# Two dilated blocks handled together, scores four blocks ahead, in a two-layer attention kernel

## The chip, the cores and the metric

The kernel runs on one core of a Trainium2 chip. The metric is device time in microseconds of one execution of the whole program. PE is TensorE (PEld its weight loads), DVE is VectorE, ACT is ScalarE, POOL is GpSimd and SP is SyncE, which issues nearly all DMAs here.

## The reference

Two layers, each with one input projection, two token mixers that read it, a gate, and one output projection. The change touches the second mixer alone: 12 heads of 64, 2048 tokens, three (window, dilation) patterns.

```
for window, dilation in ((128, 1), (512, 4), (2048, 16)):
    # queries and keys are cut into 128-token blocks per residue class of the dilation;
    # a block of queries sees its own block of keys and the one before (masked to the window)
    s = q_block @ [k_prev, k_own].T * scale ; s = where(mask, s, -inf)
    m = max(s) ; p = exp(s - m) ; l = sum(p)
    o = (p @ [v_prev, v_own]) / l ; log_den = m + log(l)
alpha = softmax(log_den over the three patterns)
od = sum(alpha * o over the three patterns) * silu(gate)
```

## The kernel before, in words

Each layer runs four stages one after the other: projection, stick-breaking mixer (`_stick`), dilated mixer (`_dilated`), output projection (`_output`, whose first loads are mixed into the end of the dilated stage). Heads are taken two at a time, so the dilated mixer has 6 pairs. A pair has 48 blocks: 16 for each pattern p. Blocks are numbered g over all pairs; t is g within its pair. In pattern 0 every block uses its own keys only (128 columns of scores, "own-key blocks"); in patterns 1 and 2 a block has 256 columns of scores unless it is the first of its residue class.

Three functions make a block:

- `front(g)`: four score matmuls on PE (L742) into one of three PSUM banks; for each of the two heads DVE adds the mask and takes the row minimum while moving the scores out of PSUM (L744), and ACT takes the exponential with its row sum (L748).
- `mid(g)`: PE transposes the weights of the block (L763; two transposes in an own-key or first block, four otherwise) into one of two PSUM banks, and one copy moves them out (L765), on ACT for one block in four, otherwise on DVE.
- `back(g0)`: for the four blocks from g0, the matmuls with the values (L777; 128x64 weights, two instructions each) into one PSUM bank, which ACT copies out (L782, L784 or L787).

The loop takes one block in each step: `front(g + 3)`, then (in later pairs) one weighting of the pair before, then `mid(g)`, and every fourth step `back(g - 4)`. `tc.keep_in_program_order` (called `pin`) fixes this order on PE. The other engines' queues are in the order that the tile framework's planner gives them; each engine then runs its queue in order.

Once a pair is done its three outputs are mixed, while the next pair runs. `stats_a` (t = 1) and `stats_b` (t = 5) turn the row minima and sums into weights for the three patterns, a chain that goes PE, ACT, DVE, POOL, ACT, POOL, DVE (a reciprocal, L832) and POOL again. `weigh(c)` spreads the weights of one sixteenth of the tokens over the partitions with one matmul (L847) and multiplies them in on DVE (L848); it runs at t = 17 to 32, one per block. After every fourth one `gate` adds the three patterns and multiplies by the gate on POOL (L855 to L858), and `put` (t = 26, 30, 34, 38) stores a quarter through SP. `load_v`, `load_k` and `load_q` bring the next data through SP, and `make_q` reorders the queries on POOL (L682, L686) for patterns 1 and 2.

The buffers that the change touches are `pe_s`, which holds the exponentials of a block between `front` and `mid` (five slots), and `ts_s`, which holds its transposes between `mid` and `back` (five slots). Scores rotate over three banks, transposes over two, weightings over two.

Of the kernel before, what the change touches and what calls it, by code (L numbers as in the profile page):

```python
# [20 lines left out]
NT = 16  # L21
NK = DM // 128
NPAIR = 6
# [468 lines left out]
def _stick(tc, mem, sq_scr, sb_scr, g_scr, mix, ident):  # L492
# [28 lines left out]
    def load_vn(pr):  # L521
        vn[pr] = mem.get(("F5", "F6")[pr], [128, NT, 128])
        nc.sync.dma_start(out=vn[pr], in_=sb_scr[:, 128 * pr:128 * pr + 128].rearrange("(j p) d -> p j d", p=128))

    def load_gt(pr):
        gt[pr] = mem.get(("F8", "F7")[pr], [128, NT, 128])
        nc.sync.dma_start(out=gt[pr], in_=g_scr[pr].rearrange("p (c a) -> p c a", c=NT))
# [62 lines left out]
    def back(u):  # L590
# [11 lines left out]
        if lo == 0 and i % 4 == 0:  # L602
# [3 lines left out]
            if i == 0:  # L606
                nc.sync.dma_start(out=mix[0][pr].rearrange("p (c a) -> p c a", c=NT), in_=gt[pr])

    LEAD, BATCH = 2, 4
    later = {2: lambda: load_gt(0), 8: lambda: load_vn(1), 12: lambda: load_gt(1),  # L610
             16: lambda: prep(1, 1), 20: lambda: prep(1, 0)}
    for u in range(LEAD):
        front(u)
    done = 0
    for u in range(len(units)):
        if u + LEAD < len(units):
            front(u + LEAD)
        mid(u)
# [12 lines left out]
def _dilated(tc, mem, v_scr, qk_scr, g_scr, mix, masks, sel, ident, neg1):  # L631
    nc = tc.nc
    pin = tc.keep_in_program_order
# [3 lines left out]
    t_r = mem.bank_ring(3, 4)  # L637
    o_r = mem.bank_ring(5)
    w_r = mem.bank_ring(6, 7)
    pa, pb = mem.get("H0", [128, 2, 2, 256]), mem.get("H1", [128, 2, 2, 256])  # L640
    ta, tb = mem.get("H6", [128, 2, 2, 2, 128]), mem.get("H7", [128, 1024])
    pe_s = Slices([pa[:, 0], pa[:, 1], pb[:, 0], pb[:, 1], tb[:, 512:1024].rearrange("p (h k) -> p h k", h=2)])
    td = mem.get("H5", [128, 2, 2, 2, 128])
    ts_s = Slices([td[:, 0], td[:, 1], ta[:, 0], ta[:, 1], tb[:, 0:512].rearrange("p (c h q) -> p c h q", c=2, h=2)])
    xa = mem.get("X", [128, 1024])
    gt_r = mem.ring("S0", "S1")
    st_r = mem.ring("T0", "T1")
# [19 lines left out]
    def load_q(pr):  # L667
        qq[pr] = [[], []]
        for h in range(2):
            t = q_r.get([128, S])  # L670
            nc.sync.dma_start(out=t, in_=qk_scr[pr, h])
            qq[pr][h].append(t)
# [33 lines left out]
    for i in range(4):  # L706
        t = gt_r.get([128, 4, 128])
# [5 lines left out]
    def geom(p, b):  # L713
        if p == 0:
            return b, 0, True
        c, n = (b // 4, b % 4) if p == 1 else (0, b)
        return c, n, n == 0

    def front(g):
        pr, p, b = g // 48, g // 16 % 3, g % 16  # L720
        if (p, b) == (0, 0):
            o3s[pr] = mem.get(f"G{pr % 2}", [128, 3, NT, 128])
            sts[pr] = st_r.get([128, 2, 3, 2, NT])
        st = sts[pr]
        c, n, first = geom(p, b)
        un = 128 if first else 256
        if p:
            run, stp = (32, 4) if p == 1 else (8, 1)
            w0 = 0 if first else run * (n - 1)
        m0 = M_OWN[p] + 128 - un  # L730
        sc = s_r.get([128, 2, 256])
        pe = pe_s.get()
        for h in range(2):
            qb = qq[pr][h][p].bitcast(F32R)[:, 128 * b:128 * b + 128]
            for s in range(2):
                kt = kk[pr][h][s]
                if p == 0:
                    kv = kt[:, 128 * b:128 * b + 128]
                else:
                    kv = kt.rearrange("p (c a) -> p c a", c=NT)[  # L740
                        :, c::stp, w0:w0 + run * un // 128].rearrange("p c (w a) -> p w c a", a=run)
                pin(nc.tensor.matmul(sc[:, h, :un], qb, kv, start=s == 0, stop=s == 1))  # L742
        for h in range(2):
            nc.vector.tensor_tensor_reduce(  # L744
                out=pe[:, h, :un], in0=sc[:, h, :un], in1=mk[:, m0:m0 + un],
                scale=-0.125, scalar=3.0e38, op0=ALU.add, op1=ALU.min,
                accum_out=st[:, 0, p, h, b:b + 1])
            nc.scalar.activation(pe[:, h, :un], pe[:, h, :un], AF.Exp, scale=-1.0,  # L748
                                 bias=st[:, 0, p, h, b:b + 1], accum_out=st[:, 1, p, h, b:b + 1])
        pes[g] = pe  # L750

    pes, tss = {}, {}

    def mid(g):
        p, b = g // 16 % 3, g % 16
        first = geom(p, b)[2]
        pe = pes.pop(g)
        tp = t_r.get([128, 2, 2, 128])
        nch = 1 if first else 2
        for ch in range(nch):  # L760
            for h in range(2):
                w = 0 if first else 1 - ch
                pin(nc.tensor.transpose(tp[:, ch, h], pe[:, h, 128 * w:128 * w + 128], ident))  # L763
        ts = ts_s.get()
        (nc.scalar.copy if g % 4 == 1 else nc.vector.tensor_copy)(ts[:, :nch], tp[:, :nch])  # L765
        tss[g] = ts

    def back(g0):
        pr, p, b0 = g0 // 48, g0 // 16 % 3, g0 % 16
        o3 = o3s[pr]  # L770
        ob = o_r.get([128, 4, 128])
        for b in range(b0, b0 + 4):
            ts = tss.pop(g0 + b - b0)
            nch = 1 if geom(p, b)[2] else 2
            for ch in range(nch):
                for h in range(2):
                    pin(nc.tensor.matmul(  # L777
                        ob[64 * h:64 * h + 64, b % 4],
                        vq[(pr * 3 + p) * 2 + (b - ch) // 8][:, (b - ch) % 8, 64 * h:64 * h + 64], ts[:, ch, h],
                        start=ch == 0, stop=ch == nch - 1))  # L780
        if p == 0:
            nc.scalar.copy(o3[:, 0, b0:b0 + 4], ob)  # L782
        elif p == 1:
            nc.scalar.copy(o3[:, 1, b0 // 4::4].rearrange("p r (n a) -> p n r a", n=4),  # L784
                           ob.rearrange("p n (r a) -> p n r a", r=4))
        else:
            nc.scalar.copy(o3[:, 2, :, 8 * b0:8 * b0 + 32].rearrange("p c (j a) -> p j c a", j=4),  # L787
                           ob.rearrange("p j (c a) -> p j c a", c=NT))
# [51 lines left out]
    def weigh(pr, c):  # L840
        o3 = o3s[pr]
        if c % 4 == 0:
            gts[pr] = gt_r.get([128, 4, 128])
            nc.sync.dma_start(out=gts[pr], in_=g_scr[2 + pr, :, 128 * c:128 * c + 512].rearrange(
                "p (c a) -> p c a", c=4))
        wb = w_r.get([128, 3, 128])
        pin(nc.tensor.matmul(wb, selr[:, c], wr, start=True, stop=True))  # L847
        nc.vector.tensor_tensor(out=o3[:, :, c], in0=o3[:, :, c], in1=wb, op=ALU.mult)  # L848

    def gate(pr, c4, m7=None):  # L850
        final = pr == NPAIR - 1
        cs = slice(4 * c4, 4 * c4 + 4)
        o3, gt = o3s[pr], gts[pr]
        e1 = nc.vector if final and c4 % 2 else nc.gpsimd
        e1.tensor_tensor(out=o3[:, 0, cs], in0=o3[:, 0, cs], in1=o3[:, 1, cs], op=ALU.add)  # L855
        e1.tensor_tensor(out=o3[:, 0, cs], in0=o3[:, 0, cs], in1=o3[:, 2, cs], op=ALU.add)
        o = o3[:, 0, cs]
        e1.tensor_tensor(out=o, in0=o, in1=gt, op=ALU.mult)  # L858
        if final:
            nc.scalar.copy(m7[0][:, cs], o)  # L860
            e1.tensor_tensor(out=m7[1][:, cs], in0=o, in1=m7[0][:, cs].bitcast(F32), op=ALU.subtract)
            if len(mix) > 1:
                put(pr, c4)

    def put(pr, c4):
        nc.sync.dma_start(out=(mix[1][0] if pr == NPAIR - 1 else mix[0][2 + pr])[:, 512 * c4:512 * c4 + 512].rearrange(
            "p (c a) -> p c a", c=4), in_=o3s[pr][:, 0, 4 * c4:4 * c4 + 4])

    LEAD = 3
    total = NPAIR * 48  # L870
    for g in range(LEAD):
        front(g)
    for g in range(total):
        pr, t = g // 48, g % 48
        if t % 8 == 2:
            load_v(g // 8 + 1)
        if t == 2:
            make_q(pr, 2)
        if pr + 1 < NPAIR:
            if t == 16:  # L880
                load_k(pr + 1)
            if t == 24:
                load_q(pr + 1)
            if t == 36:
                make_q(pr + 1, 1)
        if g + LEAD < total:
            front(g + LEAD)
        if pr and 17 <= t < 33:
            weigh(pr - 1, t - 17)
            if t % 4 == 0:  # L890
                gate(pr - 1, (t - 17) // 4)
        mid(g)
        if g % 4 == 0 and g:
            back(g - 4)
        if pr:
            if t == 1:
                stats_a(pr - 1, nc.gpsimd)
            elif t == 5:
                stats_b(pr - 1, nc.gpsimd)
            elif t in (26, 30, 34, 38):  # L900
                put(pr - 1, (t - 26) // 4)
        yield
    back(total - 4)
    m7 = [mem.get("F5", [128, NT, 128], F32R), mem.get("F6", [128, NT, 128], F32R)]
# [108 lines left out]
```

## Time and profile before

| what | value |
|---|---|
| median of 3 runs | 3153.92 us (3147.05 to 4272.47) |
| profiled execution | 3151.59 us, of which the span is 3149.9 us |
| granted TensorE clock, mean | 0.993 |
| busy share of the span | PE 97%, PEld 83%, DVE 49%, ACT 44%, POOL 37% |

The profile is one execution; the span runs from its first instruction to its last. PE's busy time counts pipelined matmuls with modelled ends, so that a full PE is not yet a PE that could go no faster. The order of work inside a stage is read from the timeline, where successive instructions of one line are merged into one row with their count.

### The profile page before, as it was taken

The page shows a single profiled execution, that of the slowest core. Times are in us where ns is not written, and L with a number is a line of the kernel's source. Part 1 is how long each engine was busy: PE and PEld are TensorE (multiplying, and loading weights), DVE is VectorE, ACT ScalarE, POOL GpSimd, SP SyncE. Part 2 cuts the span into 40 slices and gives each one's busy share as a digit, 9 for nine tenths or more (in the row PEclk, how much of TensorE's full clock was granted, in tenths as well). Part 3 has the DMA queues.
Part 4 walks back from the last instruction along what each step waited for, and adds up shares of the span by engine and source line. Part 5 has one row for each costly group of instructions (what it writes and reads, how often), then busy time and mean ns, then how long its engine had stood idle before and what let it go on. Part 6 is the DMA issues. An engine that isn't in the chain of part 4 may idle for free.

```text
span 3149.9 us, 58168 instructions
## 1 busy us (share of the span) xinstructions
PE 3069.2 (97%) x21328; PEld 2615.0 (83%) x21328; DVE 1551.8 (49%) x4035; ACT 1370.4 (44%) x3917; POOL 1170.3 (37%) x1302
## 2 busy tenths in 40 slices
PE   8999999999999999979999999999999999999799
PEld 8888888887778988868898888888877789888687
DVE  6234430013777878864253243301147778888621
ACT  5222221113667888852042122211136688888410
POOL 1056651102663445451010666511036624445500
PEclk9999999999999999989999999999999999999899
DMA  6234456417123566354343344563172236663443
GB/s 200 89 102 121 112 137 199 136 53 227 58 81 95 154 192 176 104 163 145 124 144 104 97 110 119 148 205 119 59 219 61 72 95 177 190 174 102 137 146 99
DMA packets 316891, 413.10 MB, mean 131 GB/s; under 512 B 23232, under 2 KB 248512, under 8 KB 306368
## 3 DMA queue, kind: packets, MB, share of 16 engines
q1 hardware_dynamic: 314304, 405.20, 44.0%
q10 hardware_dynamic: 2304, 4.20, 0.4%
q8 instruction: 170, 2.79, 0.4%
q14 instruction: 113, 0.93, 0.1%
HBM read 252.01 MB, written 157.29 MB: 130 GB/s over the span
## 4 chain that ended last, share of the span: by engine, by line
PE 82%; issue 6%; ACT 4%; DVE 3%; DMA 2%; POOL 2%; SPq 1%; DVEq 0%; POOLq 0%; ACTq 0%
PE b L742 8%; PE b L317 7%; PE b L316 7%; PE b L315 7%; PE b L777 6%; PE b L763 6%; PE b L321 6%; PE b L323 6%; PE b L322 6%; PE b L599 4%; PE b L967 4%; PE b L966 4%; PE b L963 4%; PE b L585 2%; PE b L558 2%
## 5 line engine op out<-in xcount | busy, mean ns | idle before, releaser
L748 ACT ACTIVATE H<-H,T 128x256 f32<-128x256 f32 (+1 forms) x1152 | 519.4, 455 | 74.3 <-DVE T L744 67.8
L744 DVE CUSTOM_DVE_ANT_0 H<-b,M 128x256 f32<-128x256 f32 (+1 forms) x1152 | 370.9, 360 | 110.7 <-PE b L742 41.5
L742 PE MATMUL b<-F,F 128*128 128x256 f32 (+1 forms) x2304 | 408.4, 301 | 3.1 <-DVE T L744 3.1
L317 PE MATMUL b<-F,F 128*128 128x512 f32 (+1 forms) x1152 | 410.0, 356 | 0.5 <-DVE F L288 0.3
L573 POOL TENSOR_TENSOR G<-G 128x512 f32<-128x512 f32 (+3 forms) x320 | 287.7, 911 | 196.5 <-DVE G L567 143.2
L567 DVE TENSOR_TENSOR_SCAN G<-G,b 128x513 f32<-128x513 f32 (+3 forms) x320 | 323.8, 1079 | 73.2 <-ACT G L566 68.1
L742 PEld LDWEIGHTS b<-F,F 128*128 128x128 f32 x2304 | 312.1, 191 | 32.1 <-issue 26.3
L763 PE MATMUL b<-ident,H 128*128 128x128 f32 x1800 | 298.8, 277 | 7.8 <-ACT H L765 5.4
L315 PE MATMUL b<-F,G 128*128 128x512 f32 (+1 forms) x768 | 275.7, 359 | 0.4 <-ACT G L287 0.4
L316 PE MATMUL b<-F,G 128*128 128x512 f32 (+1 forms) x768 | 273.6, 356 | 1.5 <-POOL F L218 1.5
L315 PE MATMUL b<-F,F 128*128 128x512 f32 (+1 forms) x768 | 274.1, 357 | 0.0
L316 PE MATMUL b<-F,F 128*128 128x512 f32 (+1 forms) x768 | 272.3, 355 | 0.0
L317 PEld LDWEIGHTS b<-F,F 128*128 128x128 f32 x1152 | 217.6, 189 | 32.2 <-DVE F L288 1.1
L765 DVE COPY H<-b 128x512 f32<-128x512 f32 (+1 forms) x432 | 241.2, 558 | 4.3 <-PE b L763 4.1
L777 PE MATMUL b<-H,H 128*64 128x128 f32 x3600 | 235.7, 278 | 0.1
L763 PEld LDWEIGHTS b<-ident,H 128*128 128x128 f32 x1800 | 212.2, 141 | 17.7 <-ACT H L765 7.7
L322 PE MATMUL b<-F,F 128*128 128x512 f32 x576 | 224.6, 390 | 0.0
L566 ACT ACTIVATE G<-b 128x512 f32<-128x512 f32 (+3 forms) x320 | 163.9, 559 | 132.3 <-PE b L559 105.9
L777 PEld LDWEIGHTS b<-H,H 128*64 128x64 f32 x3600 | 192.8, 137 | 32.2 <-issue 21.9
L748 ACT ACTIVATION_READ_ACCUMULATOR H<-H,T 128x1 f32 x1152 | 219.5, 191 | 0.0
L135 POOL TENSOR_SCALAR U<-U 128x16 f32<-128x16 f32 (+1 forms) x80 | 18.9, 236 | 536.8 <-DVE U L367 316.3
L963 PE MATMUL b<-F,H 128*128 128x512 f32 x448 | 179.4, 400 | 29.3 <-ACT H L957 29.3
(159 smaller groups left out, 6297.0 us busy)
## 6 DMA issues: line engine op xcount, KB each, us to landing
qk_l<-H SPq DMA_DIRECT2D x384, 128.0 KB
F<-qk_l SPq DMA_DIRECT2D x48, 1024.0 KB
v_l<-S SPq DMA_DIRECT2D x288, 128.0 KB
H<-v_l SPq DMA_DIRECT2D x72, 512.0 KB
F<-qk_l SPq DMA_DIRECT2D x48, 512.0 KB
sq_l<-H SPq DMA_DIRECT2D x64, 256.0 KB
g_l<-S SPq DMA_DIRECT2D x64, 256.0 KB
F<-sq_l SPq DMA_DIRECT2D x32, 512.0 KB
```

The costliest lines, as they stand in the source:

```text
L315: nc.tensor.matmul(ps, hT(q, 0, k)[:, cs], wh, start=k == 0, stop=False)
L316: nc.tensor.matmul(ps, hT(q, 0, k)[:, cs], wl, start=False, stop=False)
L317: nc.tensor.matmul(ps, hT(q, 1, k)[:, cs], wh, start=False, stop=k == NK - 1)
L322: nc.tensor.matmul(ps, wh[:, w], hT(tq, 1, k), start=False, stop=False)
L567: nc.vector.tensor_tensor_scan(out=r[:, 0:n + 1][:, ::-1], data0=g[:, 512 - n:513][:, ::-1], data1=z[:, 0:1].to_broadcast([128, n + 1]), i ...
L573: nc.gpsimd.tensor_tensor(out=b[:, :n], in0=r[:, 1:n + 1], in1=r[:, 0:n], op=ALU.subtract)
L742: pin(nc.tensor.matmul(sc[:, h, :un], qb, kv, start=s == 0, stop=s == 1))
L744: nc.vector.tensor_tensor_reduce(out=pe[:, h, :un], in0=sc[:, h, :un], in1=mk[:, m0:m0 + un], scale=-0.125, scalar=3.0e38, op0=ALU.add, op ...
L748: nc.scalar.activation(pe[:, h, :un], pe[:, h, :un], AF.Exp, scale=-1.0, bias=st[:, 0, p, h, b:b + 1], accum_out=st[:, 1, p, h, b:b + 1])
L763: pin(nc.tensor.transpose(tp[:, ch, h], pe[:, h, 128 * w:128 * w + 128], ident))
L777: pin(nc.tensor.matmul(ob[64 * h:64 * h + 64, b % 4], vq[(pr * 3 + p) * 2 + (b - ch) // 8][:, (b - ch) % 8, 64 * h:64 * h + 64], ts[:, ch, h],
L963: ins = nc.tensor.matmul(ps, h, wo[k][:, 0, ns], start=k == 0, stop=False)
```

## The change

Blocks are handled two at a time: on even g the loop now issues `front` for g + 4 and g + 5, then the weightings, then (every second time) `back(g - 4)`, then `mid` for g and g + 1. Scores thus run four blocks ahead of the transposes (LEAD 4), and the value matmuls stand ahead of the transposes. `pe_s` gets six slots and `ts_s` four. In pattern 0 the transposes of two blocks go into one bank and leave in one copy. The 16 weightings of a pair are spread over t = 16 to 36, three in four blocks (in the last pair two per two blocks, t = 18 to 32). The gates follow the weightings, and the stores move to t = 25, 31, 35, 41 (last pair: 27, 31, 35, 38).

```diff
-    pe_s = Slices([pa[:, 0], pa[:, 1], pb[:, 0], pb[:, 1], tb[:, 512:1024].rearrange("p (h k) -> p h k", h=2)])
+    pe_s = Slices([pa[:, 0], pa[:, 1], pb[:, 0], pb[:, 1]]
+                  + [tb[:, i:i + 512].rearrange("p (h k) -> p h k", h=2) for i in (0, 512)])
     td = mem.get("H5", [128, 2, 2, 2, 128])
-    ts_s = Slices([td[:, 0], td[:, 1], ta[:, 0], ta[:, 1], tb[:, 0:512].rearrange("p (c h q) -> p c h q", c=2, h=2)])
+    ts_s = Slices([td[:, 0], td[:, 1], ta[:, 0], ta[:, 1]])
...
     def mid(g):
-        p, b = g // 16 % 3, g % 16
-        first = geom(p, b)[2]
-        pe = pes.pop(g)
-        tp = t_r.get([128, 2, 2, 128])
-        nch = 1 if first else 2
-        for ch in range(nch):
-            for h in range(2):
-                w = 0 if first else 1 - ch
-                pin(nc.tensor.transpose(tp[:, ch, h], pe[:, h, 128 * w:128 * w + 128], ident))
-        ts = ts_s.get()
-        (nc.scalar.copy if g % 4 == 1 else nc.vector.tensor_copy)(ts[:, :nch], tp[:, :nch])
-        tss[g] = ts
+        both = g // 16 % 3 == 0
+        for i in range(2):
+            first = geom(g // 16 % 3, g % 16 + i)[2]
+            pe = pes.pop(g + i)
+            if i == 0 or not both:
+                tp, ts = t_r.get([128, 2, 2, 128]), ts_s.get()
+            nch = 1 if first else 2
+            lo = i if both else 0
+            for ch in range(nch):
+                for h in range(2):
+                    w = 0 if first else 1 - ch
+                    pin(nc.tensor.transpose(tp[:, lo + ch, h], pe[:, h, 128 * w:128 * w + 128], ident))
+            tss[g + i] = ts[:, lo:lo + nch]
+            if both and i == 0:
+                continue
+            on_act = g % 8 == 2 if both else (g + i) % 4 == 1
+            (nc.scalar.copy if on_act else nc.vector.tensor_copy)(ts[:, :lo + nch], tp[:, :lo + nch])
...
-    LEAD = 3
+    LEAD = 4
...
-        if g + LEAD < total:
-            front(g + LEAD)
-        if pr and 17 <= t < 33:
-            weigh(pr - 1, t - 17)
-            if t % 4 == 0:
-                gate(pr - 1, (t - 17) // 4)
-        mid(g)
-        if g % 4 == 0 and g:
-            back(g - 4)
+        if g % 2 == 0:
+            for i in (0, 1):
+                if g + LEAD + i < total:
+                    front(g + LEAD + i)
+            if pr:
+                cs = range(t - 18, t - 16) if pr == NPAIR - 1 else range(3 * (t - 16) // 4, 3 * (t - 14) // 4)
+                for c in cs:
+                    if 0 <= c < NT:
+                        weigh(pr - 1, c)
+                        if c % 4 == 3:
+                            gate(pr - 1, c // 4)
+            if g % 4 == 0 and g:
+                back(g - 4)
+            mid(g)
...
-            elif t in (26, 30, 34, 38):
-                put(pr - 1, (t - 26) // 4)
+            elif pr == NPAIR - 1 and t in (27, 31, 35, 38):
+                put(pr - 1, (t - 27) // 4 if t < 38 else 3)
+            elif pr < NPAIR - 1 and t in (25, 31, 35, 41):
+                put(pr - 1, (t - 25) // 5)
```

## Rows read from the trace of the kernel before

**Rows 1.** The page: share of the chain that ended last, by engine.
```profile
PE 82%; issue 6%; ACT 4%; DVE 3%; DMA 2%; POOL 2%; SPq 1%; DVEq 0%; POOLq 0%; ACTq 0%
```
**Rows 2.** Windows, layer 0: dilated stage, then tail; length, busy, clock, DMA, GB/s.
```profile
981.00:1374.00 393.00, 388.16 (x4030) 350.53 (x4031) 322.85 (x1452) 339.72 (x1306) 176.64 (x223) 1.00 0.54 153
1374.00:1432.00 58.00, 39.88 (x193) 31.32 (x190) 32.79 (x42) 16.10 (x24) 26.91 (x22) 0.82 0.56 178
```
**Rows 3.** Timeline of PE, first pair, pattern 1: start, length, line, count.
```profile
1006.12 1.75 PE L777 MATMUL b<-H,H 128*64 128x128 f32 x28
1007.80 0.66 PE L742 MATMUL b<-F,F 128*128 128x128 f32 x4
1008.30 0.62 PE L763 MATMUL b<-ident,H 128*128 128x128 f32 x4
1008.68 0.71 PE L742 MATMUL b<-F,F 128*128 128x256 f32 x4
...
1011.06 0.38 PE L763 MATMUL b<-ident,H 128*128 128x128 f32 x2
1011.38 0.33 PE L777 MATMUL b<-H,H 128*64 128x128 f32 x2
```
**Rows 4.** Timeline of PE, fourth pair, the same four blocks with weightings.
```profile
1203.60 1.95 PE L777 MATMUL b<-H,H 128*64 128x128 f32 x28
1205.48 0.66 PE L742 MATMUL b<-F,F 128*128 128x128 f32 x4
...
1209.76 0.33 PE L777 MATMUL b<-H,H 128*64 128x128 f32 x2
```
**Rows 5.** Timeline of PE, value matmuls in pattern 0: first pair, then fourth.
```profile
984.09 1.09 PE L777 MATMUL b<-H,H 128*64 128x128 f32 x16
987.92 1.09 PE L777 MATMUL b<-H,H 128*64 128x128 f32 x16
...
1183.27 1.09 PE L777 MATMUL b<-H,H 128*64 128x128 f32 x16
1187.91 1.10 PE L777 MATMUL b<-H,H 128*64 128x128 f32 x16
```
**Rows 6.** Windows: pattern 0 (first pair); weightings; pattern 2. Order PE PEld DVE ACT POOL.
```profile
984.10:995.90 11.80, 11.79 (x122) 10.69 (x121) 8.62 (x55) 11.80 (x56) 2.28 (x4) 1.00 0.76 194
1197.40:1216.10 18.70, 18.70 (x187) 16.77 (x186) 18.17 (x72) 14.82 (x55) 12.35 (x15) 1.00 0.55 177
1222.00:1239.00 17.00, 17.00 (x187) 16.03 (x186) 13.42 (x58) 14.92 (x55) 8.28 (x12) 1.00 0.44 137
```
**Rows 7.** Timeline of DVE and PE, third pair, where the weights are made.
```profile
1118.96 0.94 DVE L832 RECIPROCAL X<-X 32x128 f32<-32x128 f32 x1 [1.42 <-POOL X L831]
...
1120.32 0.66 PE L742 MATMUL b<-F,F 128*128 128x128 f32 x4 [0.50 <-DVE T L744]
```
**Rows 8.** Groups by form, evictions of transposes: count, busy us, mean ns, idle before.
```profile
L765 DVE COPY H<-b 128x512 f32<-128x512 f32 x228 | 156.1, 685 | 4.1 <-PE b L763 4.1
L765 DVE COPY H<-b 128x256 f32<-128x256 f32 x204 | 85.1, 417 | 0.2
L765 ACT COPY H<-b 128x512 f32<-128x512 f32 x96 | 55.3, 576 | 13.8 <-PE b L763 13.6
L765 ACT COPY H<-b 128x256 f32<-128x256 f32 x48 | 17.5, 365 | 2.4 <-PE b L763 2.4
```
**Rows 9.** Timeline of DVE, fourth pair, one block with a weighting.
```profile
1202.40 0.68 DVE L765 COPY H<-b 128x512 f32<-128x512 f32 x1
1203.00 0.41 DVE L744 CUSTOM_DVE_ANT_0 H<-b,M 128x256 f32<-128x256 f32 x1
...
1203.34 0.42 DVE L744 CUSTOM_DVE_ANT_0 H<-b,M 128x256 f32<-128x256 f32 x1
...
1203.68 0.55 DVE L848 TENSOR_TENSOR G<-G,b 128x384 f32<-128x384 f32 x1
1204.15 0.68 DVE L765 COPY H<-b 128x512 f32<-128x512 f32 x1
```

## The prediction

> **What bounds the kernel now.** I read the chain that ended last first: PE holds 82% of it, ACT 4%, DVE 3% [rows 1]. So only what shortens PE's own sequence, or a wait inside it, can move the end. The windows by stage come next: a dilated stage takes 393 us and its twin in the second layer about as long, a quarter of the span together; PE is busy 388 of the 393 at the full clock [rows 2]. Since busy PE may hide waiting, I then compared the same four blocks in a pair without weightings and in one with them, in PE's timeline. In the first pair four blocks of pattern 1 take 1011.38 - 1006.12 = 5.26 us: 1.68 from the first value matmul to the next score, 3.58 for the four steps of scores and transposes [rows 3]. With four weightings they take 6.16: 1.88 and 4.28 [rows 4]. So a weighting costs PE (4.28 - 3.58) / 4 = 0.18 us of its own, and the value matmuls lose 0.20 in their run, where they wait for the copy of the last block's transposes. DVE is why: it is busy 18.17 of 18.70 us there, against 13.42 of 17.00 in pattern 2 without weightings [rows 6].
>
> Pattern 0 is different. In the first pair four own-key blocks take 3.83 us [rows 5], and ACT is busy all 11.80 of 11.80, DVE 8.62 [rows 6]: ACT is the bound. In a later pair the same step takes 4.64, 0.81 more [rows 5]. There DVE stands in the queue before the reciprocal that waits for POOL (1.42 idle, 0.94 work), the scores behind it are not evicted, and PE waits 0.50 in one place [rows 7].
>
> So the stage is close to PE's own rate. What can be won is waits: 0.20 in four weighted groups of each later pair, 0.81 at the weights, and what ACT holds back in pattern 0. There are 2 x 6 pairs, 10 of them later ones, and 2 x 72 = 144 groups of four blocks.
>
> **The order on PE.** The numbers of scores, transposes, value matmuls and weightings stay. Each group still goes into the value matmuls once and out once, but now from scores into them and from them into transposes. The entry from transposes costs extra: two transposes take 0.32 before value matmuls, while four take 0.38 before a score, 0.19 for two; so 0.13 [rows 3]. No row shows an entry from scores. A score has 0.125 for itself already (four in 0.50 [rows 3]), so part of the handover should lie under it; ends are -0.13 (all of it) and +0.13 (as much again), that is -19 to +19 us. I take -0.05, nearer to no change than to either end: -0.05 x 144 = -7 us.
>
> The Trainium skill (TensorEngine Tiling (Array Packing), Key Properties) says that changing the tiling mode drains the engine. Scores and transposes are 128x128 and value matmuls 128x64, so by that each group pays two drains before and after, whichever neighbour stands there, and this term would be 0 and the sum 7 us later; no row of this trace has that entry.
>
> **Weightings spread.** Their 16 x 0.18 us on PE only change place. In pattern 1 a group has three instead of four, which takes 0.47 (the weighting's start to the copy's [rows 9]) from DVE: over the three groups of [rows 6] 18.17 - 1.41 = 16.76, against a PE stretch of 18.70 less 3 x 0.18 and less the waits, 17.6. That is 95% instead of 97%, so the wait shrinks but need not go. The value matmuls also come later after the transposes they read. The wait is worth at most 0.20 x 4 x 10 = 8 us; I take half, -4 (0 to -8). The last weightings now lie in pattern 2, where DVE has 3.58 of 17.00 free [rows 6] for 0.47 each.
>
> **Scores four ahead.** In pattern 0 ACT stays full. What a deeper lead gives is that PE may enter it up to a block further ahead of ACT and pay back in pattern 2, where ACT is busy 14.92 of 17.00 [rows 6]. One block is 3.83 / 4 = 0.96 us, so 0 to -11 us over 12 pairs. I take half, -6, because ACT fills the whole stretch and some of the lead will be used up by it.
>
> **The reciprocal.** DVE's queue is held as before. After the change two of three score banks are filled back to back, so PE reaches a blocked bank about as early, but the exponentials that the transposes need are older. Bounds are 0 and 0.81 x 10 = 8 us; half, -4.
>
> **Shared evictions.** Per pair ACT makes two copies of 576 ns in place of four of 365: -0.31 us, where it is the bound. DVE makes six of 685 instead of twelve of 417: -0.89 us [rows 8], which is worth nothing, DVE having 3.2 us of 11.80 free there [rows 6]. ACT's part is -4 us over 12 pairs at most; -2, as consecutive copies overlap.
>
> **Waits that are added.** The second score set of a pair needs the bank of the first block of the pair before. Between them PE runs a score set, two sets of transposes and another score set, 0.50 + 2 x 0.38 + 0.50 = 1.8 us, while DVE needs 0.68 for that block's two evictions (0.34 each [rows 9]); if it were late, all of PE would stand behind it, but it isn't unless DVE lags by over a microsecond. The sixth slot of `pe_s` and the order (value matmuls before transposes) mean that each slot's last reader stands ahead on PE of its next writer. SP: the gate loads move by at most three steps and the stores by one to three, past `load_v`, whose data is used ten blocks later. POOL: the last gate now stands behind `make_q`'s casts, and behind it the last store; the pair's output buffer is needed again only in the next pair but one. I cost these at nothing; if that cover were gone, a late load would stop the value matmuls. The tail, where PE is busy 39.88 of 58 us at clock 0.82 [rows 2], isn't touched: the last store stays at t = 38 in the last pair.
>
> Sum: -7 - 4 - 6 - 4 - 2 = -23 us on the span of 3149.9, so 3126.9; the execution is 1.7 longer than its span, and the median lies 2.3 above the profiled execution: **3131 us**, 0.7% less. The case's own range, from the bounds of its terms, is about 3115 to 3147.
>
> **Rivals.**
>
> *Waits only move (about 3154, no change).* ACT is full in pattern 0 before and after, DVE stays at 95% with the weightings, and reordering PE takes nothing off its sequence. For it: each of my terms is half of a wait. Against it: the lead is deeper everywhere. 0.17.
>
> *Slower: the copies get behind the next scores' evictions.* From a pair's last transposes to the value matmuls that read them PE has eight scores (1.0 us) and 24 of 32 value matmuls at 1.75 / 28 = 0.06 [rows 3], 1.5: about 2.6 us with a weighting. DVE needs two copies, 1.2. If the planner puts the next four score evictions (1.4) and a weighting or two (0.47 each) ahead of the second copy, it needs 3.1 to 3.5 and a start. It decides once the copy ends 2.6 us after the transposes: then some 0.7 in the 50 weighted groups and 0.2 in 36 others, +42 us, against -19 of the other terms: 3177. Against it: DVE now runs scores, weighting and copy in the program's order [rows 9], and in that order the copies come first. 0.10.
>
> *All waits go (about 3104).* Every term at its far end: -19 - 8 - 11 - 8 - 4 = -50. ACT's full stretch speaks against it. 0.08.
>
> *The shared copy is late (about 3144).* Value matmuls of the first of two own-key blocks wait for a copy that is 0.685 - 0.417 = 0.27 us longer and starts only after both blocks' transposes: 0.27 x 4 groups x 12 = +13 us on the forecast. Against it: eight scores, a microsecond, lie between. 0.05. The Trainium skill (Perfetto Trace Analysis, Optimizing Scalar/DVE Operations) points this way: where these engines aren't saturated but cause bubbles on others, it advises breaking instructions up, and this edit merges them.
>
> **How the numbers follow.** The forecast has 0.60. From 3108 to 3160 lie it, no change and the late copy, 0.82; the range leaves out the two far cases. What can be told from no change here is about 2%, 63 us: faster than 3091 would need more than every wait I found (0.02), slower than 3217 more than the slow rival with nothing won elsewhere (0.03).
>
> **What would show it.** In the changed profile a weighted group of pattern 1 should have value matmuls of 1.75 rather than 1.95, four own-key blocks of the first pair should take 3.7 to 3.8 with ACT still full, and the step after the weights should be under 4.64. The entry from scores into value matmuls can be read off PE's starts. ACT out of the bound in pattern 0, a drained PE at each pair of score sets, or DVE with copies behind the next scores would prove me wrong, and so would a planner that places the reciprocal or the output's first loads elsewhere.

## The result, and the profile after

The changed kernel takes 3193.29 us (median of 4 runs, 3188.50 to 3198.45) against 3151.56 for the kernel before on the same chip: a ratio of 1.0138, 95% interval 1.0111 to 1.0164. One of the four runs of the kernel before took 4272.47; the ratio leaves it out, so it is not the quotient of the two medians. I forecast 3131, between 3108 and 3160: wrong in direction and outside the range. The profiled execution has a span of 3188.9 us against 3149.9, so 39.0 more.

The chain of the changed kernel, by engine, and the window of its dilated stage in layer 0 (columns as in [rows 2]):

```profile
PE 86%; ACT 5%; DVE 3%; DMA 2%; issue 2%; POOL 2%; SPq 0%; DVEq 0%; ACTq 0%; POOLq 0%
```
```profile
977.00:1390.00 413.00, 388.56 (x3993) 355.70 (x3993) 317.99 (x1412) 334.52 (x1291) 176.76 (x223) 0.97 0.53 145
```

Against [rows 2] the stage is 20 us longer while PE's busy time is the same, 388.56 and 388.16: PE waits, and the granted clock is 0.97 of full instead of 1.00. The view of waits names what it waits for; engine, line, tile, releaser, then us in total, times and longest:

```profile
PE b L853 <- POOL W L842: 32.2, 6, 5.6
...
PE b L783 <- DMA H<-v_l: 3.6, 1, 3.6
...
PE b L783 <- ACT H L772: 2.0, 2, 1.0
```

The first row doesn't exist before. L853 is the weighting matmul and L842 the last step of the chain that makes the weights. To see when, I took from the timeline the time from the first value matmul of a pair to that of the next:

| pair | layer 0: before, after | layer 1: before, after |
|---|---|---|
| first | 60.22, 61.60 | 60.25, 61.59 |
| second | 66.37, **72.23** | 66.69, **72.26** |
| third | 66.67, 65.82 | 66.40, **71.99** |
| fourth | 66.38, **76.35** | 66.69, 65.83 |
| fifth | 66.68, 65.82 | 66.43, **77.60** |

Five of these pairs stall, and a sixth is the last of layer 0. The other three later pairs are 0.9 us faster than before, and the two first pairs are 1.4 slower. The five pairs of layer 0 give +15.5 us, from its sixth pair to layer 1 +7.7, the five of layer 1 +22.8, the start and the end -7.0: together the 39.0. The two longest pairs hold a second wait, in front of value matmuls: 1.74 us in the fourth pair of layer 0, and in the fifth of layer 1 the 3.6 us for a load of values that the second row above names.

The second pair, timeline of POOL, DVE and PE where its weights are made (idle time before an instruction and its releaser in brackets):

```profile
1049.14 0.45 POOL L836 TENSOR_TENSOR X<-X 32x128 f32<-32x128 f32 x1
1049.62 2.28 POOL L687 CAST F<-F 128x512 fp32r<-128x512 f32 x4
1051.86 0.45 POOL L837 TENSOR_TENSOR X<-X 32x128 f32<-32x128 f32 x1
...
1056.50 0.94 DVE L838 RECIPROCAL X<-X 32x128 f32<-32x128 f32 x1
1057.52 0.98 POOL L839 TENSOR_TENSOR X<-X 32x384 f32<-32x384 f32 x1 [5.21 <-DVE X L838]
...
1060.18 0.49 POOL L842 CAST W<-X 32x384 fp32r<-32x384 f32 x1
...
1060.73 0.69 PE L853 MATMUL b<-W,F 128*128 128x384 f32 x1 [5.62 <-POOL W L842]
```

and the same lines in the third pair, which doesn't stall:

```profile
1121.04 0.44 POOL L837 TENSOR_TENSOR X<-X 32x128 f32<-32x128 f32 x1
1121.52 0.94 DVE L838 RECIPROCAL X<-X 32x128 f32<-32x128 f32 x1 [1.25 <-POOL X L837]
...
1123.48 2.27 POOL L687 CAST F<-F 128x512 fp32r<-128x512 f32 x4
...
1127.36 0.50 POOL L842 CAST W<-X 32x384 fp32r<-32x384 f32 x1
...
1128.03 0.33 PE L853 MATMUL b<-W,F 128*128 128x384 f32 x1
```

In the stalled pair `make_q`'s four casts (L687, 2.28 us) stand between the two additions (L836, L837), and the reciprocal, whose input is ready at 1051.86 + 0.45 = 1052.31, starts only at 1056.50. The planner has put it behind the evictions of 22 blocks of the pair instead of 14; before it always stood behind 12. Why it is 22 or 23 in six of the ten pairs and 14 in four isn't shown. Meanwhile PE reaches the first weighting and waits 5.62. In the third pair the casts come later and the reciprocal waits for POOL; but the weights are ready at 1127.86, only 0.17 ahead of their use. Before, the last cast and the first weighting of the third pair were these, 1.89 apart, and as far in all ten later pairs:

```profile
1124.79 0.50 POOL L836 CAST W<-X 32x384 fp32r<-32x384 f32 x1
...
1127.18 0.39 PE L847 MATMUL b<-W,F 128*128 128x384 f32 x1
```

The Trainium skill (Perfetto Trace Analysis, Tensor Engine Instruction) says that DVE, ACT and GpSimd take their queues strictly first in, first out. The trace agrees: with the reciprocal's input ready from 1052.31, DVE stood idle until 1052.81 (0.72 us in all, 0.50 of it after the input was ready) for the copy queued ahead of it.

The wait costs more than its length, as the windows of the changed kernel before, in and after it show:

```profile
1049.60:1055.10 5.50, 5.50 (x54) 4.99 (x53) 4.47 (x27) 5.50 (x23) 2.69 (x5) 1.00 1.15 298
1055.10:1060.73 5.63, 0.01 (x1) 0.00 (x1) 2.34 (x10) 2.88 (x14) 2.95 (x4) 0.77 0.27 111
1060.73:1064.50 3.77, 3.77 (x24) 3.11 (x24) 0.98 (x2) 0.59 (x1) 0.00 (x0) 0.50 0.01 4
```

After 5.63 us without work PE is busy for 3.77 us at 0.50 of the clock, 1.2 GHz.

The other rows of before have these answers. The unweighted group of [rows 3] in the first pair, PE's timeline:

```profile
1002.84 0.69 PE L743 MATMUL b<-F,F 128*128 128x256 f32 x4
1003.45 1.75 PE L783 MATMUL b<-H,H 128*64 128x128 f32 x28
1005.13 0.87 PE L767 MATMUL b<-ident,H 128*128 128x128 f32 x6
1005.76 1.20 PE L743 MATMUL b<-F,F 128*128 128x256 f32 x8
1006.80 1.04 PE L767 MATMUL b<-ident,H 128*128 128x128 f32 x8
1007.60 1.22 PE L743 MATMUL b<-F,F 128*128 128x128 f32 x8
1008.75 1.75 PE L783 MATMUL b<-H,H 128*64 128x128 f32 x28
```

From group to group it is 5.30 us, before 5.26; the group ahead of it takes 5.24, before 5.25. Four scores take 0.61 ahead of value matmuls. Ahead of transposes they took 0.56, from 1008.68 in [rows 3] to this row of before:

```profile
1009.24 0.60 PE L763 MATMUL b<-ident,H 128*128 128x128 f32 x4
```

The 14 transposes of the group take 0.63 + 0.80 = 1.43 until the next scores; before they took 1.40, and that with 0.13 for the entry into the value matmuls. A weighted group of an undisturbed pair, for [rows 4]:

```profile
1139.79 1.75 PE L783 MATMUL b<-H,H 128*64 128x128 f32 x28
...
1143.15 0.51 PE L853 MATMUL b<-W,F 128*128 128x384 f32 x2
...
1145.34 0.34 PE L853 MATMUL b<-W,F 128*128 128x384 f32 x1
1145.61 1.75 PE L783 MATMUL b<-H,H 128*64 128x128 f32 x28
```

It takes 5.82 us with three weightings, where four had 6.16 (0.18 of the 0.34 is the weighting that moved), and its value matmuls 1.75 instead of 1.95. Value matmuls in pattern 0, first pair and then third, for [rows 5]:

```profile
979.75 0.66 PE L783 MATMUL b<-H,H 128*64 128x128 f32 x8
981.42 0.66 PE L783 MATMUL b<-H,H 128*64 128x128 f32 x8 [1.02 <-ACT H L772]
984.75 1.09 PE L783 MATMUL b<-H,H 128*64 128x128 f32 x16
988.59 1.09 PE L783 MATMUL b<-H,H 128*64 128x128 f32 x16
...
1119.48 1.09 PE L783 MATMUL b<-H,H 128*64 128x128 f32 x16
1124.15 1.04 PE L783 MATMUL b<-H,H 128*64 128x128 f32 x14
```

The first group of the first pair holds a wait of 1.02 for a shared copy on ACT (5.00 us for the group, before 3.83); the next takes 3.84; the step with the weights 4.67, before 4.64 to 4.93. ACT's evictions, by form, for [rows 8]:

```profile
L772 ACT COPY H<-b 128x512 f32<-128x512 f32 x120 | 68.7, 573 | 7.5 <-PE b L767 6.5
```

### The profile page after: what moved, and what is told of

Same layout as the page of the kernel before. It is cut to its first block, busy times and chain, and to the rows that moved or that the text cites. A ratio compares the mean times of both kernels' runs of the same rounds, so it can differ in the third digit from the quotient of the medians.

```text
span 3188.9 us, 57953 instructions
## 1 busy us (share of the span) xinstructions
PE 3069.7 (96%) x21328; PEld 2625.8 (82%) x21328; DVE 1545.7 (48%) x3963; ACT 1362.4 (43%) x3893; POOL 1172.5 (37%) x1302
## 4 chain that ended last, share of the span: by engine, by line
PE 86%; ACT 5%; DVE 3%; DMA 2%; issue 2%; POOL 2%; SPq 0%; DVEq 0%; ACTq 0%; POOLq 0%
PE b L317 9%; PE b L316 9%; PE b L315 9%; PE b L743 6%; PE b L783 6%; PE b L767 6%; PE b L321 6%; PE b L323 6%; PE b L322 5%; PE b L976 4%; PE b L980 4%; PE b L979 4%; PE b L599 4%; ACT H L749 3%; PE b L585 2%
## 5 line engine op out<-in xcount | busy, mean ns | idle before, releaser
L745 DVE CUSTOM_DVE_ANT_0 H<-b,M 128x256 f32<-128x256 f32 (+1 forms) x1152 | 353.1, 361 | 47.3 <-PE b L743 27.2
L743 PE MATMUL b<-F,F 128*128 128x256 f32 (+1 forms) x2304 | 348.2, 295 | 2.7 <-DVE T L745 2.7
L743 PEld LDWEIGHTS b<-F,F 128*128 128x128 f32 x2304 | 298.4, 194 | 5.9 <-DVE T L745 3.6
L772 DVE COPY H<-b 128x256 f32<-128x256 f32 (+1 forms) x360 | 223.3, 641 | 106.8 <-PE b L767 106.6
L767 PE MATMUL b<-ident,H 128*128 128x128 f32 x1800 | 262.5, 283 | 9.4 <-ACT H L772 8.6
L317 PEld LDWEIGHTS b<-F,F 128*128 128x128 f32 x1152 | 217.5, 189 | 31.6 <-DVE F L288 0.3
L767 PEld LDWEIGHTS b<-ident,H 128*128 128x128 f32 x1800 | 202.0, 143 | 42.5 <-issue 26.9
L783 PEld LDWEIGHTS b<-H,H 128*64 128x64 f32 x3600 | 200.9, 141 | 31.3 <-issue 15.6
```

The lines of the kernel that those rows point to most:

```text
L317: nc.tensor.matmul(ps, hT(q, 1, k)[:, cs], wh, start=False, stop=k == NK - 1)
L745: nc.vector.tensor_tensor_reduce(out=pe[:, h, :un], in0=sc[:, h, :un], in1=mk[:, m0:m0 + un], scale=-0.125, scalar=3.0e38, op0=ALU.add, op ...
L767: pin(nc.tensor.transpose(tp[:, lo + ch, h], pe[:, h, 128 * w:128 * w + 128], ident))
L783: pin(nc.tensor.matmul(ob[64 * h:64 * h + 64, b % 4], vq[(pr * 3 + p) * 2 + (b - ch) // 8][:, (b - ch) % 8, 64 * h:64 * h + 64], ts[:, ch, h],
```

## Experiments

**Theory.** The change has taken away the cover of the weights: PE comes to the first weighting earlier for the chain, and the planner's order now puts `make_q`'s casts and DVE's evictions ahead of the chain in some pairs. **Rivals.** The new order on PE, the lead, the spread or the shared evictions cost by themselves; or the reciprocal holds DVE rather than being held. "Pairs" below are later, weighted pairs other than the last of a layer, each read from the one profiled execution of its run.

**1. Casts behind the chain** (`e1_casts_behind`).

```diff
-        if t == 2:
+        if t == 6:
             make_q(pr, 2)
...
-                    eng.tensor_copy(
+                    pin(eng.tensor_copy(
```

> The changed kernel, with the casts that reorder the queries for pattern 2 pinned on POOL behind the chain that makes the weights. Theory (a late reciprocal): in 6 of the 10 later pairs the casts stand between the two additions on POOL, and the reciprocal stands on DVE behind the evictions of block 21 or 22, although the first weighting is pinned on PE right behind the scores of block 21; PE waits there, and these six pairs cost 72.2, 76.4, 72.3, 72.0, 77.6 and, the last one, 70.9 against 65.8 (last pair 62.5 before): 50 us together. Here the reciprocal stands behind block 17 in all ten: 3145 to 3160 us, no pair above 68. Rival (the pairing of blocks costs PE time by itself): nothing of that changes, about 3190. Rival (the spread of the weightings): about 3190 as well.

3146.45 us, ratio 0.9993 (0.9981 to 1.0004). The pairs take 65.8 to 66.0, one, with a wait of 2.7 us for values, 67.23. All ten reciprocals stand behind 18 blocks, and what is left of the wait is

```profile
PE b L853 <- POOL W L842: 7.1, 7, 1.2
```

So the loss is the order on the two queues of the chain; without it the change is worth about nothing.

**2. Weightings later** (`e2_weigh_later`); the casts stay where the planner puts them.

```diff
-                cs = range(t - 18, t - 16) if pr == NPAIR - 1 else range(3 * (t - 16) // 4, 3 * (t - 14) // 4)
+                cs = range(t - 24, t - 22)
...
+            elif t in (31, 35, 39, 43):
+                put(pr - 1, (t - 31) // 4)
```

> The changed kernel, with the weightings at t = 24 to 38, two for two blocks, in place of t = 16 to 36 (gates and stores follow). The reciprocal stays late on DVE in nine of ten pairs (behind block 22), but the first weighting stands behind the scores of block 29. Theory (a late reciprocal): the wait goes without the chain being any faster, 3140 to 3155 us. Rival (pairing of blocks): about 3190. Rival (the spread that starts at t = 16): 3140 to 3155 too.

3143.88 us, ratio 0.9982 (0.9973 to 0.9992), the best time measured. The pairs take 65.2 to 66.8 although nine of ten reciprocals are late, behind 23 blocks. The third pair:

```profile
1127.11 0.94 DVE L838 RECIPROCAL X<-X 32x128 f32<-32x128 f32 x1
...
1130.82 0.49 POOL L842 CAST W<-X 32x384 fp32r<-32x384 f32 x1
1134.44 0.51 PE L853 MATMUL b<-W,F 128*128 128x384 f32 x2
```

A late reciprocal costs nothing by itself; the weights are ready 3.13 us before PE asks for them.

**3. Scores two ahead** (`e3_lead_two`): `LEAD = 2` instead of 4, all else as changed.

> The changed kernel with scores two blocks ahead instead of four; blocks still in pairs, weightings still spread. The planner then puts the reciprocal behind block 11 in all ten pairs, and no casts between the additions. Theory (a late reciprocal): no wait at the first weighting; 3143 us plus what the shorter lead costs, up to some 20 us: 3143 to 3165. Rivals (pairing, or the spread of the weightings): about 3190 or more, since both stay and the lead that should help is gone.

3149.51 us, ratio 0.9998 (0.9989 to 1.0007). The reciprocal is back behind 11 or 12 blocks, no weighting waits for POOL, and pairs take 65.9 to 69.4. The first pair takes 60.2, as before the change. So the late reciprocal comes with the lead of four, and not with the pairing or the spread alone; a lead of four without the pairing wasn't run.

**4. The kernel before, with a late reciprocal** (`e4_before_late`). The end of `stats_b`, from the reciprocal on, becomes a function of its own, `stats_c`:

```diff
+        if pr and t == 16:
+            stats_c(nc.gpsimd)
...
-        nc.vector.reciprocal(mn, mn)
+        pin(nc.vector.reciprocal(mn, mn))
```

> The kernel before, one block at a time, with one thing added: the reciprocal and what follows it are issued at t = 16 and pinned on DVE behind the evictions of block 19, with the first weighting where it was, behind the scores of block 20. Theory (a late reciprocal): PE waits about 5 us at the first weighting in all ten later pairs, and some 1 us more follows: 3150 + 50 to 80 = 3200 to 3230 us. Rivals (pairing, or the spread): neither is here, so about 3150.

3203.44 us, ratio 1.0163 (1.0148 to 1.0178): nothing of the change is in this kernel but the place of one instruction of 0.94 us (what follows it in the chain has to wait for it anyway), and all ten later pairs have a group of 11.5 to 12.0. Its waits, the windows in and after one of them, and last the 30 PE instructions from the first weighting to the next value matmuls, here and in the kernel before:

```profile
PE b L853 <- POOL W L842: 36.8, 10, 3.7
```
```profile
1057.26:1062.63 5.37, 1.69 (x22) 1.38 (x21) 2.76 (x13) 3.55 (x15) 2.95 (x4) 0.92 0.55 182
1062.63:1066.00 3.37, 3.37 (x15) 3.22 (x16) 1.39 (x6) 0.95 (x2) 0.00 (x0) 0.50 0.43 177
...
1062.63:1069.26 6.63, 6.63 (x31) 6.21 (x31) 4.42 (x14) 2.77 (x9) 0.00 (x0) 0.55 0.22 90
...
1127.18:1130.99 3.81, 3.81 (x32) 3.58 (x31) 3.36 (x15) 3.40 (x14) 0.00 (x0) 1.00 0.79 254
```

(x31 and x32 count those at the windows' edges.) A wait of 3.7 us lengthens a pair by 5.4 on average (66.54 to 71.98). Behind it the same instructions take 2.3 to 2.8 us more than before, here at a clock of 0.55 over the stretch instead of 1.00; some of that comes back in the step that held the reciprocal before, now 4.1 us instead of 4.6 to 4.9.

**5. Both mends at once** (`e5_late_and_behind`): the edits of 1 and 2.

> The changed kernel with both mends: the casts for pattern 2 pinned behind the chain of the weights, and the weightings at t = 24 to 38. With the later weightings alone the best pairs take 65.2 us and some others up to 66.8, 3.6 us over it together, where the casts still stand in the chain and hold DVE. Theory (a late reciprocal and what holds it): all ten later pairs at 65.2 to 65.4, 3138 to 3142 us. Rival (the rest is not from the casts): as with the later weightings alone, 3144.

3199.63 us, ratio 1.0157 (1.0143 to 1.0171): a miss. No weighting waits, but in pairs three to five of each layer the first group takes 11.6 to 12.5. The timeline of POOL, SP's queue, ACT and PE there:

```profile
1097.62 2.29 POOL L683 CAST F<-F 128x512 fp32r<-128x512 f32 x4 [1.36 <-PE b L743]
1099.87 1.30 POOL L864 TENSOR_TENSOR G<-G,S 128x512 f32<-128x512 f32 x1
...
1101.56 6.80 SPq L872 DMA_DIRECT2D mixa_l<-G  x1
...
1118.83 0.59 ACT L788 COPY G<-b 128x512 f32<-128x512 f32 x1 [6.50 <-DMA mixa_l<-G]
...
1120.42 1.11 PE L743 MATMUL b<-F,F 128*128 128x128 f32 x4 [5.13 <-DVE T L745]
```

The last gate (L864) stands behind the next pair's casts (L683), its store (L872) behind all six loads of queries and keys (run 9's expectation says five) and one of values, and ACT's first output copy of the next pair overwrites the buffer being stored. ACT waits 6.50; the statistics' copies and DVE's minimum are queued behind it, so that the scores' evictions stop, and PE with them.

**6 and 7. The same with scores two ahead** (`e6_late_behind_lead2`), **and with no shared evictions** (`e7_late_behind_unshared`: `both = False`).

> The same two mends, with scores two blocks ahead in place of four. The prediction put 6 us (0 to 11) on the deeper lead: then 3146 us, with pattern 0 slower. Rival (the lead is worth nothing here, as pattern 0 is bound by ACT in either): as with four, 3138 to 3142; the first pair with two ahead took 3.76 to 3.84 for four own-key blocks, against 3.84 to 3.94 with four.

> The same two mends, with the own-key blocks' transposes evicted one block at a time again (two banks, one copy per block). The prediction put 2 us (0 to 4) on the shared copies: then 3142 us. Rival (the shared copy is late for the value matmuls, 0.27 us in each group of pattern 0): faster by up to 13 us, 3127 to 3135.

3146.58 us, ratio 0.9993 (0.9984 to 1.0002), with pairs of 66.0 to 66.2; and 3200.82, ratio 1.0168 (1.0154 to 1.0183), with the stalls of run 5. In the second the first pairs take 60.4 and 60.5 instead of 61.6: that is the shared copy's price with a lead of four, and in undisturbed pairs it gives back nothing (65.7, in run 5 65.65).

**8. The kernel before, weightings later** (`e8_before_weigh_later`): `weigh` at t = 24 to 39, stores at 32, 36, 40, 44.

> The kernel before, one block at a time with scores three ahead and unshared copies, with its weightings at t = 24 to 39, one per block, in place of t = 17 to 32 (gates and stores follow). If the pairing of blocks is what lets the weighted groups run without their wait of 0.2 us, this stays at 3146 to 3151. If it is enough that half of the weightings lie in pattern 2, where DVE has room, 3140 to 3146.

3153.58 us, ratio 1.0016 (1.0007 to 1.0025). Pairs 66.1 to 70.3. Later weightings alone are no gain; what run 2 has over run 8 needs the new order.

**9. Run 5 with weightings, gates and stores two blocks earlier** (`e9_earlier_gates`): `range(t - 22, t - 20)`, stores at 29, 33, 37, 41.

> The casts behind the chain as in the run with both edits (3199.6 us), but the weightings, their gates and stores two blocks earlier (from t = 22). Theory (store): in that run the last gate stands on POOL behind the next pair's casts, its store is issued at 1101.56 behind five of six loads of queries and keys, and the first output copy of the next pair waits 6.50 us for it, because it writes the buffer that is being stored. Two blocks earlier the last gate stands ahead of those casts, so that wait goes: no first group over 7 us, later pairs 65.5 to 66.5, 3140 to 3152 us. Rival (the pinned casts hold POOL, and the statistics behind it are late): the casts stand where they stood, so the first groups keep 11.5 to 12.5 us in three pairs of each layer, pairs 72 to 75, 3190 to 3205 us.

3147.46 us, ratio 0.9993 (0.9984 to 1.0001), pairs 65.5 to 65.6, no first group over 5.90. The same place:

```profile
1093.94 2.54 POOL L864 TENSOR_TENSOR G<-G,S 128x512 f32<-128x512 f32 x2
...
1096.78 2.29 POOL L683 CAST F<-F 128x512 fp32r<-128x512 f32 x4 [0.30 <-PE b L743]
...
1098.86 0.54 SPq L872 DMA_DIRECT2D mixa_l<-G  x1
```

The gates are ahead of the casts, the store ahead of the last three loads, and ACT's wait is gone: the store was the cause in run 5.

**10. Weightings later and scores two ahead** (`e10_late_lead_two`): run 2 with `LEAD = 2`.

> The changed kernel with scores two blocks ahead instead of four and the weightings from t = 24. If the lead brings nothing and only delays the reciprocal, this has the first pair of the lead of two (60.2) and the later pairs of the late weightings (65.2 to 66) with no wait for the weights: 3136 to 3146 us, below both kernels. If the lead of four gives the late weightings part of their gain, the later pairs are 66 to 68 and the time 3146 to 3156 us.

3154.60 us (3149.98 to 3169.89), ratio 1.0019 (1.0010 to 1.0028). A miss: most pairs take 65.9 to 66.4, so a lead of two costs the late weightings some 0.8 us a pair against the undisturbed pairs of run 2, and three pairs take 69 to 73. The profiled execution, the slowest of the twelve, has in one of these a wait of 4.4 us for values:

```profile
PE b L783 <- DMA H<-v_l: 8.1, 3, 4.4
```

Single waits of this kind stand in the changed kernel (3.6) and in runs 1, 2 and 8 too (2.7, 1.5 and 2.7 at the longest). Why the loads are late here and not in run 6 stays open.

**11. The spread alone** (`e11_spread_alone`): the kernel before, with

```diff
+            cs = range(t - 17, t - 16) if pr == NPAIR - 1 else range(3 * (t - 16) // 4, 3 * (t - 15) // 4)
...
+            elif pr < NPAIR - 1 and t in (25, 31, 35, 41):
```

> The kernel before with the weightings of a pair spread over 22 blocks and nothing else. Theory: the reciprocal stays behind 12 blocks of evictions, so no group over 8 us; the weighted groups of pattern 1 go from 6.19 to 5.8 or 5.9 us and those of pattern 2 with a weighting from 5.87 to 6.06: 3144 to 3152 us. Rival (the spread by itself makes the weights late): single groups of 10 us or more, 3170 to 3200 us.

3152.43 us, ratio 1.0012 (1.0003 to 1.0020). The reciprocal stays behind 12 blocks and nothing stalls, as expected; but the pattern 1 groups stay at 6.19 and a fourth of 6.58 joins them: pairs 67.2 instead of 66.4 to 66.7. The spread isn't the cause, nor a gain by itself.

**12. Weightings as dense as before** (`e12_dense_weightings`): the changed kernel with `range(t - 18, t - 16)` in every pair.

> The changed kernel with the weightings as before, four in four blocks from t = 18, so that the first stands behind the scores of t = 24 and no longer t = 22. Theory: in the pairs with the reciprocal behind 23 blocks PE still waits, by two blocks (2.9 us) less on the one side and one block later a reciprocal (1.5) on the other, so 3 to 5 us a pair in six of ten: 3165 to 3190 us. Rival (only the spread's early start, t = 16, makes PE wait): no wait for the weights, 3146 to 3156 us.

3182.02 us, ratio 1.0103 (1.0090 to 1.0116). Two blocks more cover shorten the longest wait to 4.6 us but don't remove it (27.6 us in 6 times); the pairs without a stall take 66.1 to 66.3, 0.4 more than with the spread.

## Why the prediction was wrong

**The step that failed** is "Waits that are added", costed "at nothing". It looked at banks, slots, loads, stores and gates, and not at the wait of the first weighting for its weights; and "The reciprocal" took DVE's queue "as before" and bounded its term at 0 and 8 us of gain with no loss, where the reciprocal in fact went from behind 12 blocks of evictions to behind 14, 22 or 23. That wait was readable: in all ten later pairs of before the weights were ready 1.89 us ahead of use, less than two blocks, and four engines' queues lay in the chain. Run 4 shows that the place of the reciprocal is worth +53 us in the kernel before; runs 1 and 2 take the loss off, by the order or by the cover. None of the four rivals had this mechanism. The closing sentence named it, a planner that places the reciprocal elsewhere, without a price or a chance.

**What bounds the kernel** was read rightly: only PE's sequence and the waits in it moved the end.

**The order on PE** (taken -7): nothing was won. The entry itself is cheaper, as I took it: scores ahead of value matmuls cost 0.05 (0.61 instead of 0.56), transposes 0.13. But the transposes, now behind value matmuls and in runs of six and eight, take 1.43 us a group instead of 1.27 without the entry, which I had no term for. The groups take 5.24 and 5.30 instead of 5.25 and 5.26, so between -1 and +6 us over 144 groups, within my ends. By the rule of the Trainium skill on drains (TensorEngine Tiling (Array Packing), Key Properties) the term is 0, and that was the better value.

**Weightings spread** (-4): the sign on value matmuls was right, 1.75 for 1.95. But the gain needs both edits: +0.6 a pair for the spread alone (run 11), -0.4 within the new order (run 12 against the change's 65.8), which is the 4 us over ten pairs that I took.

**Scores four ahead** (-6): a little, if anything. First pairs take 60.2 with a lead of two (runs 3 and 6), and with four 61.6, or 60.4 with unshared evictions (run 7). ACT's full stretch used up the lead: it is busy all 5.00 us of the first group. Undisturbed later pairs are 0.4 shorter with four (65.65 in run 5, 66.04 in run 6), or 0.8 with the weightings of run 2 (run 10 against it): 4 to 8 us won over ten pairs and 3 lost over two.

**The reciprocal** (-4): 4.67 against 4.64 to 4.93. A step of 3.84 comes only where the reciprocal stands later in DVE's queue (runs 1 and 9). In run 1 the next group then takes 5.5 for 4.15; in run 9, where the weightings are later too, it takes 4.1. So the 0.8 us of that step can be won by a later reciprocal with a longer cover for the weights, not by the deeper lead; of the whole pair 0.3 is left (65.55 against 65.82).

**Shared evictions** (-2): ACT's busy time fell about as worked out, 72.8 to 68.7 [rows 8], but the rival "the shared copy is late" held at one place: the first group of each layer waits 1.02. The Trainium skill (Perfetto Trace Analysis, Optimizing Scalar/DVE Operations) advises breaking up instructions that cause bubbles on other engines where ScalarE and VectorE aren't saturated. Run 7, which breaks the copies up, wins 1.1 to 1.2 us per layer there, though ACT, on which the late copy stood, was full.

**Loads and the store** (nothing): a load of values did come late once in the profiled execution, 3.6 us. For the store the cost was right in the changed kernel, where ACT never waits for one, but not the reason: the last gate stands ahead of `make_q`'s next casts there (1097.26 and 1101.60 in the second pair), not behind them. Run 5, which has it behind them, lost the cover.

Without the stalls a later pair is 0.6 to 0.9 us shorter and the first 1.4 longer: for ten pairs of the one and two of the other that is about -7 + 3 = -4 us, not -23. Runs 1 and 9, at 0.9993, agree. That is nearer to the rival "Waits only move" than to the forecast.

## What to carry to other kernels

Where a few small instructions on several engines make the operand of a matmul whose place is fixed, measure how long that operand is ready ahead of its use, in every repetition, and treat any edit that moves either end as a possible stall. If a planner orders the queues between them, the margin has to cover its worst order, or the chain has to be written into the order. A mend that delays one thing delays what is queued behind it: give the late end (here the gates, the store and the buffer) the same look.

## What the runs showed of the hardware

A wait on PE went on costing after its end: behind idle times of 3.7 and 5.6 us the granted clock was 0.50 for more than 3 us of full work, and 30 PE instructions that took 3.81 us at 1.00 took 6.63 behind a wait of 3.7. And one store, issued behind seven loads of the same queue, held ACT until 17 us after its issue (1101.56 to 1118.83, run 5), where in run 9, with three of the loads of queries and keys behind it, it held nobody.
